# Decay tables, scores and outputs of the retention layer, placed later in the first layer of a two-block transformer

## The chip, the cores and the metric

The kernel runs on one core of one Trainium2 chip. The time is the device time of one execution in microseconds (us), from start to end, without the host. TensorE multiplies matrices into PSUM, VectorE (DVE in the profile) and ScalarE (ACT) work element by element, GpSimd (POOL) does small powers here, and SyncE (SP) issues the DMA loads.

## The reference

Two transformer blocks on 256 rows of 1024 values. Only the first layer of the first block matters here: a retention layer with 6 heads and a memory attention with 4 heads beside it.

```python
h = rms_norm(x, attn_norm_w[layer])
u = h @ w_in[layer]
q, k, v, g = ...                       # 6 heads: q, k 64 wide, v 128 wide, gates 768 wide
o = rms_norm(retention(q, k, v), ret_gn_w[j])
o_main = jax.nn.silu(g) * o.reshape(B, S, MAIN_WIDTH)
...
mkv = memn @ w_mem_kv[layer]           # memory keys and values from a normed memory of 256 rows
o_mem = memory_attention(qc, mk, mv).reshape(B, S, MEM_WIDTH)
x = x + jnp.concatenate([o_main, o_mem], axis=-1) @ w_out[layer]
```

Retention is written in chunks in the reference. The kernel uses its closed form: scores q·k of each head, times a table of decays (powers of that head's gamma by distance, zero where a later chunk is masked), times v. The gates pass a SiLU. Then come a feed-forward network, a second layer with differential attention, and a second block of other mixers.

## The kernel before, in words

All products are made in parts: `unit` loads a weight block of 256 rows (a DMA into a `raw` buffer, of which there are three), ScalarE casts it to a rounded high half `hi` (L328), VectorE subtracts to get the low half `lo` (L213 is the helper `tt`), with four buffers each. `proj` multiplies a block in two half-blocks of six products each (12 products of 512 columns for a block of 512 columns), and before each half-block it calls `tick()`, which moves every running side chain (a Python generator, begun by `start`) one step on. `drain` runs a chain to its end. So the code's order of small work is set by the ticks of the projection beside which it runs. The order in which an engine's instructions are issued in the end is a planner's: it follows the code's order, but a later instruction whose data and buffers are ready can go ahead of an earlier one that waits.

The first layer, `ret_layer`, goes like this. The query/key projection of retention (`proj_T`, columns 0 to 767, in two parts) leaves three tiles of tag T. `setup_rest` loads the remaining constants and x. Then, in the version before, six decay tables of 128 x 384 values (192 KB each) are fetched from the array `small` into tiles of tag L (22 buffers) by `fetch` (L209). The first value projection (columns 768 to 1279) follows; its two results are written by ScalarE into L tiles. The transposed memory, memT, comes in four loads into tiles of tag V (L456; three buffers), each with a scaling into halves (`early`). The second value projection (1280 to 1535) has the memory queries in the same blocks. Beside it runs `products`: for each head two products q·k into one PSUM tile (four such tiles, two tags in turn), and a multiplication with the table on VectorE, in place in the L tile. Both chains are drained behind it.

Next comes `mem_kv(0)`, the memory's key/value projection, and beside it `outputs`: for four groups (two row halves, two sets of three heads) the scores times v into a PSUM tile, a square (ScalarE), a sum, two small steps around a power on GpSimd, and a scaling into a T tile. It is drained, and the gate projections follow (columns 1536 to 2303, four blocks of 512 columns, four of 256); beside them `memory` finishes the key transposes after seven ticks and then makes the memory attention (query transposes, logits, softmax, transposes of the probabilities, values). The gates are multiplied with the outputs, transposed, and go with the memory's result into the output projection; before it, the second layer's memory projection is made, `mem_kv(1)`.

Of the kernel before, what the change touches and what calls it, by code (L numbers as in the profile page):

```python
# [128 lines left out]
class _Builder:  # L129
# [490 lines left out]
    def ret_layer(self):  # L620
        nc, w = self.nc, self.a['w_in'][0]
        hT = self.scaled_T(self.a['xT'], 'attn', 'H')
        qk = []
        for cols in ([(0, 512)], [(512, 256)]):
            for ps in self.proj_T(hT, w, cols):
                e = self.t('T', F32, (P, 2, S))
                (nc.scalar.copy if len(qk) % 2 else nc.vector.tensor_copy)(e, ps)
                qk.append(e)
        self.setup_rest()
        dec = []  # L630
        for h in range(6):
            d = self.t('L')
            self.fetch(d[:, :384], f'dec{h}')
            dec.append(d[:, :384])
        dT = []

        def products():
            for h in range(6):
                s = slice((h % 2) * 64, (h % 2) * 64 + 64)
                f = h // 2  # L640
                q, k = qk[f // 2][s, f % 2, :], qk[(3 + f) // 2][s, (3 + f) % 2, :]
                ps = self.psum()
                self.mm(ps[:, :S], k[:, :P], q)
                self.mm(ps[:, S:S + P], k[:, P:], q[:, P:])
                self.tt(dec[h], ps[:, :384], dec[h])
                dT.append(dec[h])
                if h % 2:
                    yield

        v = [[None, None] for _ in range(2)]  # L650
        a0 = self.proj(hT, w, [(768, 512)])
        ms, r = self.stats(self.x)
        epsms, hr, rv = self.tiny(2), self.tiny(2), self.tiny(2)
        self.ts(epsms, ms, EPS)
        self.ts(hr, r, 0.5)
        self.stt(rv, r, 64.0 ** -0.5, r)
        for t in range(2):
            v[t][0] = self.t('L')
            self.act(v[t][0], a0[t], AF.Copy, scale=rv[:, t:t + 1])
        self.msums = []  # L660
        self.memT = self.scaled_T(self.a['memT'], 'mem', 'Z', self.msums)

        def early():
            for k in range(0, 8, 2):
                yield
                yield
                self.memT[k]

        ea = self.start(early())
        pr = self.start(products())  # L670
        a1 = self.proj(hT, w, [(1280, 256), (2304, 256)])
        for t in range(2):
            v[t][1] = self.t('L')
            self.act(v[t][1][:, :S], a1[t][:, :S], AF.Copy, scale=rv[:, t:t + 1])
        qn = self.mem_q([a1[t][:, S:] for t in range(2)], epsms)
        self.drain(pr, ea)
        on = {}

        def outputs():
            yield  # L680
            last = None
            for t in range(2):
                for hg in range(2):
                    o = self.psum()
                    for hh in range(3):
                        h = hg * 3 + hh
                        for j in range(t + 1):
                            blk = (0 if t == 0 else (P if j == 0 else S))
                            self.mm(o[:, hh * P:(hh + 1) * P], dT[h][:, blk:blk + P],
                                    v[j][h // 4][:, (h % 4) * P:(h % 4 + 1) * P], start=(j == 0), stop=(j == t))  # L690
                    rr = self.head_rms(o[:, :384], 3, P, epsms[:, t:t + 1])
                    if last:
                        last()

                    def last(t=t, hg=hg, o=o, rr=rr):
                        self.ts(rr, rr, hr[:, t:t + 1])
                        e = self.t()
                        self.tt(self.h3(e[:, :384], P), self.h3(o[:, :384], P), self.bc(rr, P))
                        on[t, hg] = e
                    yield  # L700
                    yield
            last()

        out = self.start(outputs())
        mkv0, omT = [], []
        kv = self.mem_kv(0, mkv0)
        self.drain(out)

        def memory():
            yield from kv  # L710
            yield
            yield from self.mem_attn(qn, mkv0, omT)

        mem = self.start(memory())
        sg = {}
        for c, wd in ((0, 512), (1, 256)):
            g = self.proj(hT, w, [(1536 + c * 512, wd)])
            for t in range(2):
                e = self.t('Z')
                self.act(e[:, :wd], g[t], AF.Tanh, scale=hr[:, t:t + 1])  # L720
                self.stt(e[:, :wd], e[:, :wd], 1.0, g[t], ALU.add, ALU.mult)
                sg[t, c] = e
        og = [[None] * 6 for _ in range(2)]
        for t in range(2):
            for hg in range(2):
                e = on[t, hg]
                for lo, hi, c in (((0, 3, 0),) if hg == 0 else ((3, 4, 0), (4, 6, 1))):
                    d = e[:, (lo - 3 * hg) * P:(hi - 3 * hg) * P]
                    base = lo * P - c * 512
                    self.tt(d, d, sg[t, c][:, base:base + (hi - lo) * P])  # L730
                for h in range(3):
                    og[t][hg * 3 + h] = e[:, h * P:(h + 1) * P]
        oT = []

        def transposes():
            yield
            yield from self.to_T(oT, lambda t, f: og[t][f], 6, 'L', lambda f: self.col('ret', f))

        tr = self.start(transposes())
        self.mkv1 = []  # L740
        kv = self.mem_kv(1, self.mkv1)
        self.drain(tr, mem)
        self.start(kv)
        self.xT = self.out_proj(oT + omT, self.a['w_out'][0], order=[6, 7, 0, 1, 2, 3, 4, 5], gname='ffn')
# [949 lines left out]
```

## Time and profile before

| what | value |
|---|---|
| median of 3 runs | 1261.44 us (1261.12 to 1261.72) |
| profiled execution, device time | 1263.25 us |
| profiled execution, span from the first to the last instruction | 1261.5 us |
| TensorE busy | 1239.2 us (98%) |
| VectorE / ScalarE / GpSimd busy | 858.9 / 687.3 / 60.9 us |
| mean granted clock of TensorE | 0.998 |

The times are of runs without a profile, the span and the busy times of the one with. A granted clock of 1.00 is TensorE's 2.4 GHz level, 0.50 its 1.2 GHz level.

### The profile page before, as it was taken

The numbers are of one execution on the slowest core, as the hardware profiler recorded it, in microseconds if no ns is written. First come the engines' busy times: TensorE is split into PE (matmuls) and PEld (weight loads), VectorE is DVE, ScalarE is ACT, GpSimd is POOL, SyncE is SP. The second block draws the span as 40 slices with busy tenths as digits, with TensorE's granted clock in tenths as the row PEclk, the third lists the DMA queues.
The fourth block names the chain that finished last, engine by engine and source line by source line (L and its number), as shares of the span: only waits on it lengthen the run. The fifth ranks groups of instructions, "written<-read, shape, count | busy, mean of one in ns | idle before, by whom it ended". The sixth has DMA issues, their size and how long they took to land.

```text
span 1261.5 us, 18951 instructions
## 1 busy us (share of the span) xinstructions
PE 1239.2 (98%) x7128; PEld 1060.6 (84%) x7128; DVE 858.9 (68%) x1370; ACT 687.3 (54%) x1087; POOL 60.9 (5%) x63
## 2 busy tenths in 40 slices
PE   8999999999999999999999999999999999999997
PEld 7888888888778888888888998878888898888886
DVE  6777777755798677775558896676646665777553
ACT  5655655544576475554466973623554454655442
POOL 0110000000220100000000100111000000000000
PEclk9999999999999999999999999999999999999999
DMA  8745566655554356665663454332666543555662
GB/s 299 227 127 174 171 196 185 190 199 185 182 163 152 121 170 196 186 192 192 192 190 100 149 153 145 116 98 86 182 186 188 176 151 117 177 190 184 189 195 101
DMA packets 146573, 213.62 MB, mean 169 GB/s; under 512 B 15536, under 2 KB 71984, under 8 KB 146480
## 3 DMA queue, kind: packets, MB, share of 16 engines
q1 hardware_dynamic: 145904, 211.34, 53.4%
q8 instruction: 56, 0.92, 0.3%
q0 software_dynamic: 144, 0.52, 0.1%
q10 hardware_dynamic: 432, 0.53, 0.1%
q14 instruction: 37, 0.30, 0.1%
HBM read 210.92 MB, written 1.44 MB: 168 GB/s over the span
## 4 chain that ended last, share of the span: by engine, by line
PE 81%; DVE 8%; DMA 4%; ACT 3%; issue 2%; POOL 1%; SPq 0%; POOLq 0%; DVEq 0%; ACTq 0%
PE acc L235 73%; PE ps L235 6%; DMA raw<-in_w_in_dram 3%; DVE lo L213 2%; PE ps L238 2%; POOL tiny L228 1%; DVE Z L220 1%; ACT T L223 1%; ACT hi L328 1%; DVE T L213 1%; DMA V<-in_mem_2T_dram 1%; ACT L223 0%; DVE tiny L217 0%; DMA T<-dr 0%; DVE L L213 0%
## 5 line engine op out<-in xcount | busy, mean ns | idle before, releaser
L213 DVE TENSOR_TENSOR lo<-raw,hi 128x1024 fp32r<-128x1024 f32 (+1 forms) x393 | 474.4, 1210 | 286.9 <-ACT hi L328 285.9
L328 ACT CAST hi<-raw 128x1024 fp32r<-128x1024 f32 (+1 forms) x393 | 408.3, 1040 | 400.7 <-PE acc L235 322.3
L235 PE MATMUL acc<-H,hi 128*128 128x512 f32 (+1 forms) x1696 | 471.6, 348 | 1.7 <-ACT hi L328 0.9
L235 PE MATMUL acc<-H,lo 128*128 128x256 f32 x1328 | 369.5, 280 | 3.4 <-DVE lo L213 3.4
L235 PEld LDWEIGHTS acc<-H,hi 128*128 128x128 f32 x1696 | 294.6, 189 | 47.5 <-ACT hi L328 1.6
L235 PEld LDWEIGHTS acc<-H,lo 128*128 128x128 f32 x1328 | 250.4, 189 | 5.3 <-DVE lo L213 4.7
L235 PE MATMUL acc<-hi,H 128*128 128x512 f32 (+1 forms) x672 | 217.4, 395 | 0.8 <-ACT hi L328 0.8
L235 PE MATMUL acc<-hi,Z 128*128 128x512 f32 x544 | 175.5, 395 | 0.1
L235 PE MATMUL acc<-hi,L 128*128 128x512 f32 x512 | 160.7, 391 | 0.0
L235 PEld LDWEIGHTS acc<-hi,H 128*128 128x128 f32 x672 | 125.4, 189 | 28.2 <-issue 2.8
L235 PE MATMUL acc<-lo,H 128*128 128x512 f32 (+1 forms) x336 | 131.2, 390 | 0.0
L235 PEld LDWEIGHTS acc<-hi,Z 128*128 128x128 f32 x544 | 102.1, 188 | 21.1 <-ACT Z L249 0.5
L235 PEld LDWEIGHTS acc<-hi,L 128*128 128x128 f32 x512 | 96.1, 188 | 19.8
L235 PE MATMUL acc<-lo,Z 128*128 128x512 f32 x272 | 106.4, 391 | 0.0
L235 PE MATMUL acc<-lo,L 128*128 128x512 f32 x256 | 99.7, 389 | 0.0
L228 POOL TENSOR_TENSOR tiny<-tiny,constants 128x2 f32<-128x2 f32 (+4 forms) x41 | 45.3, 1109 | 978.8 <-DVE tiny L217 903.6
L235 PEld LDWEIGHTS acc<-lo,H 128*128 128x128 f32 x336 | 63.8, 190 | 12.1 <-issue 0.7
L235 PEld LDWEIGHTS acc<-lo,Z 128*128 128x128 f32 x272 | 51.2, 188 | 9.8
L235 PEld LDWEIGHTS acc<-lo,L 128*128 128x128 f32 x256 | 48.1, 188 | 9.7
L414 ACT COPY T<-acc 128x256 f32<-128x256 f32 x120 | 44.2, 369 | 14.4 <-PE acc L235 11.2
L213 DVE TENSOR_TENSOR T<-acc,T 128x256 f32<-128x256 f32 x120 | 44.9, 415 | 0.0
L223 ACT ACTIVATE H<-ps,constants 128x256 fp32r<-128x256 f32 x56 | 24.6, 471 | 12.8 <-DVE H L220 9.8
(224 smaller groups left out, 1052.8 us busy)
## 6 DMA issues: line engine op xcount, KB each, us to landing
raw<-in_w_in_dram SPq DMA_DIRECT2D x91, 512.0 KB, 3.6
raw<-in_w_gate_up_dram SPq DMA_DIRECT2D x176, 256.0 KB, 3.2
raw<-in_mlp_w_dram SPq DMA_DIRECT2D x64, 512.0 KB, 3.7
raw<-in_w_down_dram SPq DMA_DIRECT2D x44, 512.0 KB, 3.6
raw<-in_w_out_dram SPq DMA_DIRECT2D x24, 512.0 KB, 3.7
raw<-in_w_in_dram SPq DMA_DIRECT2D x42, 256.0 KB, 3.6
raw<-in_w_mem_kv_dram SPq DMA_DIRECT2D x8, 512.0 KB, 4.2
raw<-in_xattn_wk_dram SPq DMA_DIRECT2D x8, 512.0 KB, 4.5
```

The source lines that it names most:

```text
L213: return (eng or self.nc.vector).tensor_tensor(out=out, in0=a, in1=b, op=op)
L220: self.nc.vector.scalar_tensor_tensor(out=out, in0=a, scalar=s, in1=b, op0=op0, op1=op1)
L223: self.nc.scalar.activation(out, in_, f, scale=scale, bias=bias, **k)
L228: self.nc.gpsimd.tensor_tensor(out=out, in0=in_, in1=self.c('mhalf')[:, :n], op=ALU.pow)
L235: self.nc.tensor.matmul(out, lhsT, rhs, start=start, stop=stop, skip_group_check=True)
L238: self.nc.tensor.transpose(out, in_, self.ident[:in_.shape[0], :in_.shape[0]])
L328: nc.scalar.copy(hi[:, k, :W], raw[:, k, :W])
L414: self.nc.scalar.copy(out[:, a, :], accs[a][:, 1, :])
```

## The change

The fetches of the six tables move behind the second value projection and the memory queries. The scores (`products`) no longer run beside the second value projection but beside `mem_kv(0)`. The outputs no longer run beside `mem_kv(0)` but, started behind it, beside the gate projections, and are drained after these. No instruction is added or removed.

```diff
         self.setup_rest()
-        dec = []
-        for h in range(6):
-            d = self.t('L')
-            self.fetch(d[:, :384], f'dec{h}')
-            dec.append(d[:, :384])
-        dT = []
+        dec, dT = [], []
...
         ea = self.start(early())
-        pr = self.start(products())
         a1 = self.proj(hT, w, [(1280, 256), (2304, 256)])
...
         qn = self.mem_q([a1[t][:, S:] for t in range(2)], epsms)
-        self.drain(pr, ea)
+        self.drain(ea)
+        for h in range(6):
+            d = self.t('L')
+            self.fetch(d[:, :384], f'dec{h}')
+            dec.append(d[:, :384])
...
-        out = self.start(outputs())
+        pr = self.start(products())
         mkv0, omT = [], []
         kv = self.mem_kv(0, mkv0)
-        self.drain(out)
+        self.drain(pr)
+        out = self.start(outputs())
...
                 sg[t, c] = e
+        self.drain(out)
```

## Rows read from the trace of the kernel before

**Rows 1.** The page, part 1: busy time, share of the span, instructions.
```profile
PE 1239.2 (98%) x7128; PEld 1060.6 (84%) x7128; DVE 858.9 (68%) x1370; ACT 687.3 (54%) x1087; POOL 60.9 (5%) x63
```
**Rows 2.** Busy time by stretch: length, each engine, granted clock, DMA share, GB/s.
```profile
16.00:24.78 8.78, 8.78 (x75) 8.65 (x74) 3.47 (x10) 4.87 (x12) 0.70 (x1) 1.00 1.05 371
24.78:29.91 5.13, 4.37 (x29) 3.35 (x29) 4.55 (x8) 2.38 (x3) 0.00 (x0) 1.00 0.88 326
29.91:33.32 3.41, 3.41 (x10) 2.64 (x9) 3.41 (x6) 3.29 (x7) 0.00 (x0) 0.50 0.76 193
33.32:52.30 18.98, 18.98 (x85) 15.73 (x84) 11.82 (x14) 11.67 (x16) 0.00 (x0) 1.00 0.77 237
52.30:67.96 15.66, 15.66 (x91) 13.59 (x90) 13.21 (x28) 8.45 (x15) 6.47 (x5) 1.00 0.51 160
67.96:79.81 11.85, 11.85 (x58) 9.80 (x58) 6.95 (x18) 4.50 (x9) 3.53 (x4) 1.00 0.36 109
79.81:89.71 9.90, 8.60 (x71) 7.74 (x69) 9.18 (x23) 6.56 (x18) 0.00 (x0) 1.00 0.42 129
```
**Rows 3.** Timeline of TensorE, 24.75 to 33.4 us: start, duration, instruction, idle before.
```profile
24.78 2.48 PE L235 MATMUL ps<-T,T 64*128 64x256 f32 x20
28.02 0.73 PE L235 MATMUL acc<-hi,H 128*128 128x512 f32 x2 [0.76 <-ACT hi L328]
28.69 0.92 PE L235 MATMUL ps<-T,T 64*128 64x256 f32 x4
...
33.25 0.44 PE L235 MATMUL acc<-hi,H 128*128 128x512 f32 x1
```
**Rows 4.** Timeline of ScalarE, 21 to 30 us.
```profile
26.93 1.04 ACT L328 CAST hi<-raw 128x1024 fp32r<-128x1024 f32 x1 [4.57 <-DMA raw<-in_w_in_dram]
28.27 1.05 ACT L328 CAST hi<-raw 128x1024 fp32r<-128x1024 f32 x1 [0.30 <-DMA raw<-in_w_in_dram]
```
**Rows 5.** Timeline of the SP queue, 16 to 34 us.
```profile
16.23 4.42 SPq L209 DMA_DIRECT2D L<-in_small_dram  x6
21.10 2.20 SPq L322 DMA_DIRECT2D raw<-in_w_in_dram  x3
```
**Rows 6.** The fetches of L209 between 15 and 30 us, the decay tables.
```profile
DMA to landing us min/median/max: 5.2/6.5/6.7
```
**Rows 7.** Timeline of the SP queue, 48 to 54 us.
```profile
50.33 2.95 SPq L322 DMA_DIRECT2D raw<-in_w_in_dram  x2
53.33 0.46 SPq L456 DMA_DIRECT2D V<-in_memT_dram  x1
```
**Rows 8.** Timeline of ScalarE, 50 to 54 us.
```profile
52.77 0.47 ACT L223 ACTIVATE L<-acc,tiny 128x256 f32<-128x256 f32 x1 [0.50 <-PE acc L235]
53.14 0.38 ACT L223 ACTIVATE V<-acc 128x256 f32<-128x256 f32 x1
```
**Rows 9.** Groups of VectorE by shape, 16 to 33.4 us: count, busy us, mean ns.
```profile
L213 DVE TENSOR_TENSOR lo<-raw,hi 128x1024 fp32r<-128x1024 f32 x3 | 3.6, 1217 | 0.3 <-ACT hi L328 0.3
L213 DVE TENSOR_TENSOR L<-ps,L 128x384 f32<-128x384 f32 x6 | 3.0, 550 | 0.2 <-PE ps L235 0.2
...
L627 DVE COPY T<-acc 128x512 f32<-128x512 f32 x2 | 1.4, 692 | 3.3 <-PE acc L235 3.3
```
**Rows 10.** The fetch of L209 at 250.7 us, a load alone.
```profile
DMA to landing us min/median/max: 3.6/3.6/3.6
```
**Rows 11.** Groups by shape, 52.3 to 67.96 us: the outputs' work.
```profile
L235 PE MATMUL ps<-L,L 128*128 128x128 f32 x36 | 4.7, 274 | 0.0
...
L469 DVE TENSOR_REDUCE tiny<-V 128x3 f32<-128x384 f32 x4 | 2.2, 545 | 0.0
...
L213 DVE TENSOR_TENSOR T<-ps,tiny 128x384 f32<-128x384 f32 x3 | 1.7, 552 | 0.0
L217 DVE TENSOR_SCALAR tiny<-tiny,tiny 128x3 f32<-128x3 f32 x6 | 1.2, 226 | 0.8 <-POOL tiny L228 0.8
```
**Rows 12.** Waits of TensorE, 67.96 to 92 us: us in total, times, longest.
```profile
PE ps L238 <- DVE T L217: 1.0, 1, 1.0
```

## Prediction

> **What bounds the kernel now.** I read the page first. TensorE is busy 98% of the span, VectorE 68% [rows 1], so a change can only win where TensorE waits or is slowed, and only lose where it makes TensorE wait. The table of stretches then shows where, around this change. Before 24.78 us the second query/key projection runs without a hole while the DMA engines are full (share 1.05). From 24.78 to 29.91 TensorE is busy 4.37 of 5.13 us, and from 29.91 to 33.32 its granted clock is 0.50, the 1.2 GHz level. From 33.32 to 79.81 nothing is idle, and from 79.81 to 89.71 it is busy 8.60 of 9.90 [rows 2].
>
> The timeline of TensorE shows the bad stretch in detail. The scores of heads 0 to 4 (20 instructions) fill it from 24.78, then TensorE idles 0.76 us; two products of the value projection start at 28.02, head 5's scores at 28.69, and only at 33.25 does the projection run at its later pace [rows 3]. What is late is the first weight block of that projection: ScalarE's cast of it starts at 26.93, after 4.57 us of waiting for its DMA; the next one follows 1.34 us later [rows 4]. The SP queue says why it is late: after the last constants, the six decay tables are issued (4.42 us for the six issues), and the three weight blocks only from 21.10 on [rows 5]. Each table takes 5.2 to 6.7 us to land [rows 6].
>
> How much is lost there? Of the 8.47 us from 24.78 to 33.25, the scores hold TensorE for 2.48 and 0.92 [rows 3]. Eleven projection products fit before 33.25; at the pace of the next stretch, 85 instructions in 18.98 us or 0.223 each [rows 2], they would need 2.46. So 5.86 us of work took 8.47: **2.61 us are lost**. 0.76 of it is the idle time; the 3.41 us at half clock give up to half of themselves, 1.70; the rest, 0.15, is changes between kinds of work.
>
> **The change, part by part.** *Tables.* Whether they really load later is a matter of buffers: they need no data. The code takes them from tag L, now behind the four value tiles of that tag. In this trace a tile seems to get a buffer only after every earlier tile of its tag has one: the last quarter of memT (tag V) is issued at 53.33 [rows 7], just after ScalarE began, at 53.14, the second of two V tiles that stand before it in the code [rows 8], though SP had been free for it earlier. By that, no table can be issued before the last value tile is written, now 52.77 [rows 8].
>
> Six tables of 192 KB, at 1.34 us for a 512 KB block [rows 4], are 6 x 0.50 = 3.0 us of DMA time, taken out from before the first value block. Its cast then starts at 23.9 instead of 26.93, and ends after 1.05 at 24.95. The low half takes VectorE 1.22 us [rows 9], so it is there at 26.2, or 26.9 if the copy of the last query/key tile (0.69) [rows 9] goes first. TensorE is free at 24.78, so it waits 0.2, does the two products that need no low half (0.45, to 25.4), and has a hole of 0.8 to 1.5 us. The scores need no table, only VectorE's multiplication behind them does, so the first four heads can fill the hole as they fill it now (they took 2 x 0.78 us, below). Hole with filling 0.1, without 1.5; with the first 0.2 I take 0.3 lost. Nothing is then late: the blocks land 1.34 apart and each feeds 12 products, 2.7 us. No half clock follows, since the holes that came before it are gone. Head 5 runs alone now, 0.92; if head 4 does too, the other two pairs take (2.48 - 0.92) / 2 = 0.78 each. Heads 4 and 5 as a pair would save 2 x 0.92 - 0.78 = 1.06; I take 0.4, since they may be split again. Startup gain: 2.61 - 0.3 + 0.4 = **2.7 us**, between 1.1 (hole of 1.5 unfilled, no pairing) and 3.5.
>
> *Scores and tables in the memory key/value stage (52.30 to 67.96).* VectorE's six multiplications of 0.55 [rows 9] move here, 3.3 us, while the outputs' work, below, leaves; VectorE was busy 13.21 of 15.66 [rows 2], so it has room. On SP the six issues go behind the memory weights; gate blocks are issued from 50.33 [rows 7] and first used at 67.96, so 3.0 us of DMA time more is hidden. Were that cover gone, it would cost up to those 3.0. The new wait: heads 4 and 5 need a score buffer back, there are four, and these are released by the multiplication with a table. A table issued at the last value tile, 0.5 us into the stage, lands 3.6 us later at best (a load from the same array that runs alone [rows 10]) or 6.7 at worst [rows 6]; with 0.55 more, 4.6 to 7.7 into the stage. The code puts heads 4 and 5 at the third half-block, 12 x 0.223 = 2.7 into it. Left there, TensorE would stand 1.9 to 5.0. The order of issue follows readiness, as head 5's place behind two projection products shows [rows 3]; the error to be feared is that of a misjudged landing, as the 0.76 us at 28.02. I take 0.4, with bounds 0 and 5.0.
>
> *Outputs into the gates (67.96 to 89.71).* The 36 small products (4.7 us of TensorE) and, for each of four groups, a square on ScalarE, and a reduction (0.55), two small steps (0.23 each) and a multiplication (0.55) on VectorE [rows 11], move from one full stage to another. TensorE's part costs the same in either. VectorE's part is 4 x 1.56 = 6.2 us; VectorE is busy 6.95 of 11.85 and then 9.18 of 9.90 [rows 2], and the stage grows by 4.7, so it fits, if it comes early. The code puts the groups at every second half-block, the last of them one step before memory attention's transposes. There VectorE is crowded, and TensorE's wait of 1.04 us for the softmax scaling [rows 12] is already VectorE's doing. The last group, 1.56 us, falls into this crowd; about as much there, the gate multiplications, can wait, and the second memory projection's blocks can fill a hole of TensorE. Best, the present 1.04 is filled; worst, all 6.2 us push the attention. I take 0.1 lost.
>
> Sum: -2.7 + 0.4 + 0.1 = **-2.2 us**. It is made against the profiled execution, span 1261.5 and time 1263.25, which lies 1.8 above the median 1261.44 of the runs without profile. I put the same difference on the median: **1259.2 us**. This is just short of 0.2% (2.5 us), about what a measurement of this kernel can tell from no change.
>
> **A rule against the change.** The table of six landings above 5 us, at a DMA share of 1.05, says that loads issued early here take turns from the weights [rows 2, 6]. The Trainium skill, DMA: Bandwidth & Descriptors, section Rules for kernel authors, says the opposite of what the change does: issue a DMA early, compute, and wait on it late, so that its fixed cost overlaps. By that rule the gain would be eaten by the wait for tables; that is the second rival, and the sum would be +0.4 instead of -2.2.
>
> **Rivals.**
> 1. *The gates' hole closes too.* The startup gain stays 2.7, no wait for tables comes, and the 1.04 us before the softmax transposes are filled: -3.7, 1257.7, between -3.2 and -4.2 by how heads 4 and 5 fall. For it: TensorE's pending work there grows. Against: VectorE's queue there has no idle share to speak of. Chance 0.15.
> 2. *The tables come late.* TensorE reaches heads 4 and 5 and stands 1.9 to 5.0 us, middle 3.0: -2.7 + 3.0 + 0.1 = +0.4, 1261.8, between 1260.7 and 1263.8. For it: the distance between 2.7 and 4.6 us. Against: the order so far followed readiness. Chance 0.08.
> 3. *The tables don't move.* Buffers of L are free early; if my reading of rows 7 and 8 is wrong, SP issues the tables where it does now and nothing at the start changes: 1261.4, within 0.5. Chance 0.09.
> 4. *Slower: VectorE's queue in the gates.* Its place is the chain from the last output group through key copy, query copy and the softmax's reductions to the transposes TensorE waits for. Every group of 1.56 us that runs there instead of earlier lengthens that wait; two groups undo the gain, and with all four it is 6.2 - 2.7 = +3.5, 1264.9. For it: 9.18 of 9.90 busy. Against: the first groups come eight half-blocks earlier. Chance 0.06.
>
> **How the numbers follow.** The forecast has 0.62, with its own range of -1.0 to -3.4 (1258.0 to 1260.4); its part beyond -2.5 is 0.28. Faster: 0.28 + 0.15 = 0.43. Within 0.2%: the other 0.34 + 0.08 + 0.09 = 0.51. Slower: 0.06. The range for 8 in 10 runs from 1257.2 (first rival's far end) to 1262.0 (third rival, and the second's lower half); outside are the fourth, half of the second, and tails.
>
> **What would show it.** Right: the timeline of SP has the tables behind the memory weights, near 48 us; the cast of the first value block starts near 24; no stretch near 30 us has a granted clock of 0.50; the gates begin earlier and end about 2 us earlier. Wrong: tables still at 16 us; TensorE waits for a table-fed multiplication in the key/value stage; the wait for the softmax scaling grows past 2 us, or the granted clock halves elsewhere.

## The result and the profile after

The changed kernel takes 1270.25 us (median of 6, 1267.42 to 1273.83), the kernel before 1261.65 in the same comparison (6 runs): ratio 1.0068, interval 1.0057 to 1.0079, so 8.6 us slower. The forecast was 1259.2 with a range up to 1262.0, and 0.06 for slower. The profiled execution took 1269.07 us, its span is 1267.4. Of the six runs, the three slowest (1271.43 to 1273.83) show a mean granted clock of 0.993 to 0.994, the other three, the profiled one among them, 0.996 to 0.997.

The windows of the kernel after, in the columns of [rows 2], cut at its own stages: the start of the first value projection, the memory key/value stage (49.42 to 70.33), the gates (70.33 to 98.36).

```profile
25.83:33.30 7.47, 7.47 (x34) 5.67 (x33) 6.27 (x10) 5.69 (x9) 0.00 (x0) 1.00 0.93 313
33.30:49.42 16.12, 16.12 (x74) 13.06 (x72) 10.22 (x11) 10.73 (x16) 0.00 (x0) 1.00 0.76 229
49.42:58.95 9.53, 6.09 (x30) 4.44 (x30) 5.38 (x13) 3.60 (x7) 2.50 (x2) 1.00 0.90 298
58.95:65.78 6.83, 6.83 (x18) 4.80 (x17) 4.07 (x8) 1.04 (x1) 0.00 (x0) 0.50 0.18 43
65.78:70.33 4.55, 4.55 (x21) 3.73 (x20) 2.23 (x3) 1.44 (x2) 0.00 (x0) 1.00 0.34 120
70.33:86.65 16.32, 16.32 (x97) 14.22 (x96) 10.24 (x27) 6.62 (x13) 6.18 (x6) 1.00 0.27 82
86.65:98.36 11.71, 8.77 (x71) 8.01 (x69) 10.45 (x27) 6.58 (x18) 0.85 (x1) 1.00 0.39 111
```

The start is what the prediction wanted: no idle time, clock at 1.00, where [rows 2] have 0.76 us idle and 3.41 us at 0.50. The key/value stage is where it went wrong: 3.44 us idle and 6.83 us at half clock, of which about half, 3.4, is lost (an estimate: the work in it would have taken half the time at 1.00). The gates have 2.94 us idle, against 1.30 in [rows 2]. The timeline of TensorE shows the place in the key/value stage.

```profile
51.02 0.93 PE L235 MATMUL ps<-T,T 64*128 64x256 f32 x8
...
53.59 0.39 PE L235 MATMUL acc<-lo,Z 128*128 128x512 f32 x1
57.42 0.92 PE L235 MATMUL ps<-T,T 64*128 64x256 f32 x4 [3.44 <-DVE L L213]
58.27 0.73 PE L235 MATMUL acc<-hi,Z 128*128 128x512 f32 x2
58.84 0.53 PE L235 MATMUL acc<-lo,Z 128*128 128x512 f32 x1
```

The releaser is VectorE's line 213 on an L tile, the multiplication with a table. So the next question is why that came at 57. The timeline of the SP queue, and then the view of line 209 in this stretch, with the landing times of its six fetches:

```profile
47.29 2.80 SPq L322 DMA_DIRECT2D raw<-in_w_in_dram  x2
50.13 0.46 SPq L456 DMA_DIRECT2D V<-in_memT_dram  x1
50.65 3.10 SPq L209 DMA_DIRECT2D L<-in_small_dram  x6
```
```profile
DMA to landing us min/median/max: 5.6/5.7/5.8
```

And VectorE, then ScalarE, in the same stretch:

```profile
56.42 0.48 DVE L220 SCALAR_TENSOR_TENSOR Z<-V,constants,Z 128x256 fp32r<-128x256 f32 x1 [4.08 <-ACT Z L223]
56.82 0.55 DVE L213 TENSOR_TENSOR L<-ps,L 128x384 f32<-128x384 f32 x1
```
```profile
55.88 0.91 ACT L223 ACTIVATE Z<-V,constants 128x256 fp32r<-128x256 f32 x2 [5.22 <-DMA V<-in_memT_dram]
```

The tables did move, as the reading of [rows 7, 8] had it: behind the last quarter of memT, 50.65 in place of 16.23 [rows 5]. The first lands at 50.65 + 5.7 = 56.35. VectorE's first multiplication starts at 56.82, because its in-order queue also stood for memT's last quarter; without that it could have started some 0.5 earlier. It ends at 57.37, TensorE goes on at 57.42. The two things behind the wait are nearly equal in time, and the tables are enough for it. In the stage's own time, the first table was there 6.9 us after its start (the prediction had 4.1 to 7.2 for that) and TensorE was through with all that stood ahead of head 4's scores at 4.6 (53.98). The prediction had 2.7 for that: it counted twelve products of the projection and left out the scores of heads 2 and 3 (0.93 us at 51.02).

### The profile page after: what moved, and what is told of

Same layout as the page of the kernel before. It is cut to its first block, busy times and chain, and to the rows that moved or that the text cites. A ratio compares the mean times of both kernels' runs of the same rounds, so it can differ in the third digit from the quotient of the medians.

```text
span 1267.4 us, 18955 instructions
## 1 busy us (share of the span) xinstructions
PE 1242.4 (98%) x7128; PEld 1063.2 (84%) x7128; DVE 859.0 (68%) x1370; ACT 688.0 (54%) x1087; POOL 60.3 (5%) x63
## 4 chain that ended last, share of the span: by engine, by line
PE 82%; DVE 7%; DMA 4%; ACT 3%; issue 2%; POOL 1%; SPq 0%; POOLq 0%; ACTq 0%; DVEq 0%
PE acc L235 74%; PE ps L235 6%; PE ps L238 2%; DVE lo L213 2%; DMA raw<-in_w_in_dram 2%; POOL tiny L228 1%; ACT hi L328 1%; DVE T L213 1%; DVE Z L220 1%; ACT T L223 1%; DMA V<-in_memT_dram 0%; DVE tiny L217 0%; DMA raw<-in_w_mem_kv_dram 0%; DVE L L213 0%; DMA T<-dr 0%
## 5 line engine op out<-in xcount | busy, mean ns | idle before, releaser
L213 DVE TENSOR_TENSOR lo<-raw,hi 128x1024 fp32r<-128x1024 f32 (+1 forms) x393 | 474.5, 1210 | 285.6 <-ACT hi L328 284.6
L213 DVE TENSOR_TENSOR T<-acc,T 128x256 f32<-128x256 f32 x120 | 44.9, 416 | 0.0
```

The costliest lines, as they stand in the source:

```text
L213: return (eng or self.nc.vector).tensor_tensor(out=out, in0=a, in1=b, op=op)
```

## The experiments

Four kernels separate the three moves; the rest measure single terms. All differences are medians against the kernel before in the same comparison (1260.79 to 1261.91).

### The three moves, taken apart

Outputs beside the gates alone, in the kernel before:

```diff
-        out = self.start(outputs())
...
-        self.drain(out)
+        out = self.start(outputs())
...
+        self.drain(out)
```

> The kernel before with one part of the change: the outputs run beside the gates; tables and scores stay early. Theory A (the loss is the wait for the tables in the key/value stage and the half clock behind it, the gates only add what the changed kernel's two waits there, 2.21 and 0.74 us against 0.25 and 1.04, show): about 1.7 us slower than before, no wait over 1 us between 45 and 70 us. Rival B (the outputs beside the gates are the main cause): 5 us or more slower. The prediction's own term: 0.1 us.

Measured: 1263.95, +2.7 us, 1.0022 [1.0012, 1.0031].

The changed kernel with its tables fetched behind the results of the first value projection:

```diff
             self.act(v[t][0], a0[t], AF.Copy, scale=rv[:, t:t + 1])
+        for h in range(6):
+            d = self.t('L')
+            self.fetch(d[:, :384], f'dec{h}')
+            dec.append(d[:, :384])
         self.msums = []
...
         self.drain(ea)
-        for h in range(6):
-            d = self.t('L')
-            self.fetch(d[:, :384], f'dec{h}')
-            dec.append(d[:, :384])
```

> The changed kernel, with the table fetches one projection earlier, behind the results of the first value projection, so that they should be issued near 38 us instead of 50.65. Theory A: the 3.44 us wait of TensorE and the 6.83 us at half clock both go, the startup gain of about 2 stays, the gates' 1.7 stay: within 1 us of before. Rival B: still 4 us or more slower than before. Rival C (late is not the tables but the last quarter of memT, on which ScalarE waits 5.22 us and behind which the multiplications are queued): the wait near 57 us stays above 2 us.

Measured: 1263.55, +2.3, 1.0018 [1.0010, 1.0027].

The kernel before with only that: tables behind the first value projection, scores and outputs as before:

> The kernel before with the table fetches alone moved behind the results of the first value projection; scores and outputs stay where they were. Theory A: the startup gain without its prices, 2 us faster than before (2.7 by the prediction's term); the cast of the first value block starts near 24 us. If the startup stall was not made by the tables: same as before within 0.5 us.

Measured: 1264.33, +3.1, 1.0025 [1.0016, 1.0034]. A miss: it was to be faster.

The changed kernel with the tables fetched where they were before:

> The changed kernel, with the table fetches back at their old place before the first value projection. Theory A: no wait near 57 us, the startup stall back, the gates' price: 1.5 to 2.5 us slower than before. Rival D (the scores beside the memory projection cost by themselves, by their place and the clock): 4 us or more slower.

Measured: 1262.74, +1.5, 1.0011 [1.0003, 1.0019]. In its trace the scores did not move: with the tables there early, the planner has them at the start, where they were before.

```profile
25.62 2.48 PE L235 MATMUL ps<-T,T 64*128 64x256 f32 x20
```

So this kernel differs from the one before by the outputs alone, and the reading that scores beside the memory projection cost by themselves is not put to the test by it. The kernel with the tables behind the first value projection has them beside the memory projection.

These put the 8.6 us together: tables fetched behind the second value projection instead of the first, 8.6 - 2.3 = **6.3**; behind the first instead of at the start, which moves the scores too, 2.3 - 1.5 = **0.8** (the two intervals overlap, so this is not told from nothing); everything else, which is the outputs in the gates, **1.5** (2.7 by the first of these kernels; the intervals overlap). In the waits of TensorE from 24 to 100 us, of the changed kernel and then of the one with the tables behind the first value projection, the wait for L213 is there and gone, while that for L529 stays:

```profile
PE ps L235 <- DVE L L213: 3.4, 1, 3.4
PE ps L235 <- DVE T L529: 2.2, 1, 2.2
PE ps L238 <- DVE T L217: 0.7, 1, 0.7
```
```profile
PE ps L235 <- DVE T L529: 2.9, 1, 2.9
PE ps L238 <- DVE T L217: 0.7, 1, 0.7
PE ps L235 <- ACT T L559: 0.2, 1, 0.2
```

3.44 us of wait and 3.4 lost at half clock are 6.8 by the profile, 6.3 by the runs. The profile is of an execution 1.2 us below the changed kernel's median; where the slower runs have their further half clock isn't known. The kernel with only the tables moved shows the same wait once more, where its scores stand, and half clock behind it (3.41 us, 45.51 to 48.92); its wait:

```profile
PE ps L235 <- DVE L L213: 2.3, 1, 2.3
```

The wait and half of the 3.41 us are 4.0, more than the 3.1 that it lost; so its start may have gained about 0.9, an estimate from one profile.

In the kernels with all of it moved and earlier tables, memT's last quarter is issued later than in the changed one (51.50 with the tables behind the first value projection, 52.72 with them at the start, against 50.13), and there is no such wait. So memT is not its cause.

### The wait for the tables by itself

The changed kernel, tables as late as ever, the scores of heads 4 and 5 three half-blocks later:

```diff
                 if h % 2:
                     yield
+                if h == 3:
+                    for _ in range(3):
+                        yield
```

> The changed kernel with the scores of heads 4 and 5 put three half-blocks later, behind tables that land as late as before. If what costs most is TensorE standing at those scores because their buffers come free only with the first multiplications with a table: the wait of 3.4 us falls below 1 us, no half clock follows in the memory key/value stage, and the time falls by 4 to 6 us to 1264 to 1266. If instead the late memory load and VectorE's queue behind the tables hold the projection itself, the wait moves to one of its products and the time stays at 1268 or above.

Measured: 1265.74 (6 runs, 1263.99 to 1266.99), +4.6, so 4.0 us less than the change's 8.6. The waits:

```profile
PE ps L235 <- DVE T L529: 2.7, 1, 2.7
PE ps L235 <- DVE L L213: 0.4, 1, 0.4
```

The wait shrank from 3.4 to 0.4 and the half clock in this stage is gone, with the tables as late (issued from 50.42 on, 50.65 in the changed kernel). Between 53.98, where the changed kernel stands, and 57.02 TensorE ran products of the projection without idle time, so there was other work that was ready:

```profile
56.70 0.39 PE L235 MATMUL acc<-hi,Z 128*128 128x512 f32 x1
57.02 0.92 PE L235 MATMUL ps<-T,T 64*128 64x256 f32 x4
```

What was wrong was the distance between scores and tables. It stays 2.3 us above the kernel with the earlier tables; in its profiled execution two stretches of 3.41 us at half clock stand later (85.08 and 754.09), at up to 1.7 us each; whether that is so in its other runs isn't known.

### What the start was worth

The kernel before without the table loads:

```diff
-            self.fetch(d[:, :384], f'dec{h}')
+            nc.gpsimd.memset(d[:, :384], 1.0)
```

> The kernel before with the six tables set to 1.0 by GpSimd in place of being loaded, so the decay weighting is left out; everything else stays. It gives the most that freeing the start from the table loads can bring, with the scores where they are. By the prediction's startup term (idle 0.76 plus 1.70 of half clock plus 0.15): 2 to 2.6 us faster than before, 1258.6 to 1259.2. By the rival reading that the half clock near 30 us belonged to the one profiled execution (two kernels with the same start show 0.43 and 0.48 us idle and the clock at 1.00 there): 0.3 to 0.8 us faster, 1260.4 to 1260.9, no idle ahead of the first value product.

Measured: 1260.00 against 1261.17, 0.9992 [0.9983, 1.0000]: 1.2 us faster by the medians, 1.0 by the ratio, by the interval between 0 and 2.1. And the kernel before with the fetches one weight block later, called from inside the first value projection:

```diff
+        def tables():
+            for h in range(6):
...
-        a0 = self.proj(hT, w, [(768, 512)])
+        a0 = self.proj(hT, w, [(768, 512)], meanwhile=tables)
```

> The kernel before with the six table loads one place later in the code: behind the first weight block of the first value projection instead of ahead of it. Scores and outputs stay. If the idle time ahead of that projection (0.4 to 0.8 us) is all that can be had at the start, and the scores fill it as they come: no idle there, 0.4 to 1.0 us faster than before, 1260.2 to 1260.8, the same as without any table loads (1260.0). If the second and third block now come late behind the tables, or the scores wait for them as they did with tables behind the whole projection: a new wait of 1 to 2.5 us between 27 and 36 us, and 1261.5 to 1264.

Measured: 1261.13 against 1260.79, 1.0001 [0.9992, 1.0010]. Its start has no idle time and no half clock in the profile, and the scores no new wait; still nothing is gained. Part of the reason is seen in kernels whose start is the same as before's. The window from the scores on, in the kernel with the outputs moved alone, then in the changed one with early tables:

```profile
25.76:33.50 7.74, 7.26 (x41) 5.75 (x41) 7.44 (x12) 5.31 (x8) 0.00 (x0) 1.00 0.73 246
```
```profile
25.62:33.30 7.68, 7.25 (x41) 5.75 (x41) 7.42 (x12) 5.28 (x8) 0.00 (x0) 1.00 0.72 247
```

The clock is 1.00 in both, the idle time 0.48 and 0.43. Over the eleven profiles with tables loaded early, that of before among them, half clock stands at the start in three. So the 1.70 us belonged to some executions, and the profiled one, 1.8 us above the median, was one of these. The other two lie 1.0 and 2.4 us above the medians of their kernels.

The idle time saved is also paid back: scores that filled the start's hole go into a stage without one. With early tables the 24 products took 2.48 + 0.92 = 3.40 us in two groups [rows 3]; in the kernel with tables behind the first value projection they are in four groups, 0.70 + 0.92 + 0.93 + 1.51 = 4.06:

```profile
26.09 0.70 PE L235 MATMUL ps<-T,T 64*128 64x256 f32 x2
...
48.27 0.92 PE L235 MATMUL ps<-T,T 64*128 64x128 f32 x6
...
50.71 0.93 PE L235 MATMUL ps<-T,T 64*128 64x256 f32 x8
...
53.27 1.51 PE L235 MATMUL ps<-T,T 64*128 64x256 f32 x8
```

0.66 us more against 0.43 saved, and at the end of the key/value stage this kernel is 0.65 us later than the one with early tables (63.01 and 62.36), though its value projection began 3.1 earlier (25.45 and 28.54). The groups account for 0.23 of that; the rest isn't traced. Nor is the number of groups the whole of it: eight products took 0.93 at 50.71 and 1.51 at 53.27.

### What the outputs cost beside the gates

The wait that grew is the one for L529, VectorE's copy of the transposed queries, ahead of the logits. In VectorE's timeline of the changed kernel:

```profile
87.90 0.22 DVE L217 TENSOR_SCALAR tiny<-tiny,tiny 128x3 f32<-128x3 f32 x1
88.03 0.28 DVE L213 TENSOR_TENSOR T<-T,Z 128x128 f32<-128x128 f32 x1
89.08 0.23 DVE L217 TENSOR_SCALAR tiny<-tiny,tiny 128x3 f32<-128x3 f32 x1 [0.77 <-POOL tiny L228]
89.22 0.68 DVE L529 COPY T<-ps 128x512 f32<-128x512 f32 x1
```

What it copies is there well before, since TensorE's transposes of the queries end at 86.90:

```profile
86.30 0.60 PE L238 MATMUL ps<-constants,Z 128*128 128x128 f32 x4
```

The copy stands behind the last output group's second small step, which waits for GpSimd's power. To take the copy out of this queue, it goes to ScalarE (`nc.scalar.copy` in `mem_attn`), in the kernel before as a control and in the changed one with early tables:

> The kernel before with one instruction moved: the copy of the transposed memory queries out of PSUM goes from VectorE to ScalarE. It is the control for the next kernel. TensorE waits 0.25 us ahead of the logits there, so at most 0.3 us faster; the wait for the softmax scaling (1.0 us) is VectorE's and stays: 1260.9 to 1261.4.

> The changed kernel with its tables loaded at the old early place (1262.74 us, TensorE waits 2.2 us ahead of the logits) and the same one copy on ScalarE. If the outputs in the gates cost what they cost because VectorE reaches that copy late, behind the outputs' small steps and their round trip to GpSimd: the wait falls below 1 us and the time by 1.5 to 3 us, to 1259.7 to 1261.2. If the wait is for something else (the key copy, ScalarE's own queue, the outputs' buffers), it stays above 1.5 us and so does the time, 1262 to 1263.5.

Measured: 1261.26 (+0.1, as expected) and 1262.35 (+1.2, against +1.5 with the copy on VectorE: no gain that can be told). In the second the waits ahead of the logits fell to 0.4 and 0.3, but the wait for the softmax scaling came in their place:

```profile
PE ps L238 <- DVE T L217: 1.5, 1, 1.5
PE acc L235 <- ACT hi L328: 0.8, 1, 0.8
PE ps L235 <- DVE tiny L217: 0.4, 1, 0.4
PE ps L235 <- DVE T L213: 0.3, 1, 0.3
```

So the copy is where VectorE's lateness shows first, and not its cause. Next, the groups one half-block apart, to have them over before the crowd (one `yield` less in `outputs`), with early tables and with tables behind the first value projection:

> The changed kernel with its tables loaded at the old early place (1262.74 us), and the four output groups one half-block apart in the gates instead of two, so that the last of them stands some four half-blocks earlier. If the cost of the outputs in the gates is that the last groups fall into VectorE's crowd just ahead of the memory attention: TensorE's wait ahead of the logits falls from 2.2 us to about the 0.25 us of the kernel before, and the time by 1 to 2 us, to 1260.7 to 1261.7. If the stage is simply too full for VectorE wherever they stand, the waits and the time stay, 1262 to 1263.5.

> The same closer outputs in the kernel whose tables are loaded behind the first value projection (1263.55 us; waits of 2.9 and 0.75 us in the gates). The same two readings: 1261.3 to 1262.5 if the place of the last groups is the cost, 1263 to 1264.5 if it is the amount. It is the best form that the change can have with tables behind a value projection; if the startup gain of the prediction (2.7 us) were real on top, it would reach 1259 to 1260.

Measured: 1265.06 (+4.3) and 1265.48 (+4.7). Both readings missed: it got 2.4 to 2.8 us worse. The last group's products did come earlier in the first of them (71.24 in place of 75.16), but VectorE's copy came later (82.40 in place of 81.25). Its timeline shows it standing for GpSimd in each group:

```profile
73.32 0.23 DVE L217 TENSOR_SCALAR tiny<-tiny,tiny 128x3 f32<-128x3 f32 x1 [0.96 <-POOL tiny L228]
...
75.96 0.23 DVE L217 TENSOR_SCALAR tiny<-tiny,tiny 128x3 f32<-128x3 f32 x1 [1.03 <-POOL tiny L228]
...
79.14 0.23 DVE L217 TENSOR_SCALAR tiny<-tiny,tiny 128x3 f32<-128x3 f32 x1 [0.96 <-POOL tiny L228]
```

These waits are 3.9 us in all, against 3.7 with the groups two half-blocks apart, so they don't tell why closer is worse.

So the power was left out (`head_rms` then returns the mean square itself), in the kernel with early tables and in the one with closer groups:

```diff
-                    rr = self.head_rms(o[:, :384], 3, P, epsms[:, t:t + 1])
+                    rr = self.head_rms(o[:, :384], 3, P, epsms[:, t:t + 1], False)
```

> The changed kernel with its tables loaded at the old early place (1262.74 us), and the power of the outputs' norm on GpSimd left out: the outputs are scaled by their mean square instead of its inverse root. One small GpSimd step of 0.85 us in each of the four groups goes, and VectorE no longer waits for it (3.7 us in all in the gates, against 1.4 in the kernel before). If these waits at the head of VectorE's queue are what makes the outputs dear in the gates: the wait ahead of the logits falls from 2.2 us to below 1 and the time by 1 to 2 us, to 1260.7 to 1261.7, the kernel before's. If it is the amount of VectorE's own work, waits and time stay at 1262 to 1263.5.

> The kernel with the outputs one half-block apart (1265.06 us), and the same power left out. If VectorE's waits for GpSimd are why standing closer made it slower (3.02 us ahead of the logits): 2.5 to 4.5 us faster, 1260.5 to 1262.5, and then closer is no worse than two half-blocks apart. If closer is worse because more of VectorE's work is due at once: at most 1 us faster, 1264 to 1265.

Measured: 1260.99 (-0.9 against before; 0.9989 [0.9980, 0.9998]) and 1260.77 (-1.1; 0.9997 [0.9988, 1.0006]), 2.4 and 5.4 us under the kernels with the power by medians, 2.8 and 4.7 by the ratios. Neither has a wait for L529 any more; the first one's waits are

```profile
PE ps L238 <- DVE T L217: 0.7, 1, 0.7
PE acc L235 <- ACT hi L328: 0.3, 1, 0.3
```

VectorE has as much work of its own as with the power, so it is the waits for the power that make the outputs dear there, at either distance. Last, the same without leaving anything out: the row's factor is folded into the step ahead of the power, so that VectorE meets the power's result one instruction later, at the scaling.

```diff
+        self.ts(c1, ms, 4.0 / P)
+        self.stt(c2, ms, 4.0 * EPS, ms)
...
-        self.ts(ss, ss, 1.0 / d, ALU.mult, epsms, ALU.add)
+        self.ts(ss, ss, 1.0 / d if scale is None else scale, ALU.mult, epsms, ALU.add)
...
-                    rr = self.head_rms(o[:, :384], 3, P, epsms[:, t:t + 1])
+                    rr = self.head_rms(o[:, :384], 3, P, c2[:, t:t + 1], c1[:, t:t + 1])
...
-                        self.ts(rr, rr, hr[:, t:t + 1])
```

> The changed kernel with its tables loaded at the old early place, and the outputs' last small step on VectorE (the factor 0.5/rms of the row, behind GpSimd's power) folded into the step before the power by scaling the mean square and its epsilon by the row's constants; the result is the same. VectorE then meets GpSimd's power only at the scaling of the outputs, a group later. If standing at the head of the queue is the cost: like the kernel without the power, 1 to 2.5 us under its 1262.74 us, 1260.2 to 1261.7, and no wait above 1 us ahead of the logits. If the planner puts the scaling where it must wait as well: 1262 to 1263.

> The kernel before with the same fold. There the outputs stand in the memory key/value stage, where VectorE's waits for GpSimd (1.4 us in all) are covered by TensorE's full queue. If it is the place that makes them dear: no change against the kernel before, within 0.5 us. If four small steps fewer are worth something by themselves: 0.5 to 1.5 us faster.

> The kernel with the outputs one half-block apart (1265.06 us) and the same fold. If VectorE's stand for GpSimd is the cost: 2.5 to 4.5 us faster, 1260.5 to 1262.5, like the same kernel without the power. If the scaling, now due one half-block behind its power, takes over the wait: 1263 to 1265.

Measured: 1261.08 (+0.2, 1.0006 [0.9997, 1.0015]), 1261.48 (+0.6, 1.0008 [0.9999, 1.0016]) and 1262.48 (+1.6, 1.0011 [1.0002, 1.0019]). Beside the gates the fold brings the outputs down to what the kernel before takes; where they stood before it brings nothing. With closer groups it helps by 2.7 us and leaves a wait of 2.5 ahead of the logits: there the scaling takes over the stand. VectorE's waits for GpSimd with L213, from 62 to 100 us, without the power, then with the fold (groups two half-blocks apart), then with fold and closer groups:

```profile
DVE T L213 <- POOL tiny L228: 1.7, 2, 0.9
```
```profile
DVE T L213 <- POOL tiny L228: 4.6, 5, 1.0
```
```profile
DVE T L213 <- POOL tiny L228: 5.6, 6, 1.0
```

So with the fold and the wider distance VectorE still stands 2.9 us at three of the four scalings, and yet the cost is gone: TensorE's wait for the copy is 0.7 in place of 2.2. What went is the last group's stand of 0.77 right ahead of the copy, and four small steps; the copy starts at 79.60, in place of 81.25. With closer groups all four scalings stand ahead of the copy. No kernel that computes the whole came out below the kernel before.

## Why the prediction was wrong

**Where the tables go** (buffers of tag L, SP's order) was right, to the instruction in front of them. The rival in which they don't move fell.

**The tables' wait, "I take 0.4", is the step that failed.** The bounds were right: "Left there, TensorE would stand 1.9 to 5.0" and it stood 3.44, in part by luck: it came to the scores 4.6 us into the stage, not 2.7, and went on at 8.0, not at 4.6 to 7.7. What was wrong is the choice inside them: "The order of issue follows readiness". On the chip it did not: TensorE stood at these scores while products of the projection were ready, as the kernel with the later scores shows. The order is the planner's; what it took the tables' landing to be isn't on record. In the changed kernel and in the one with only the tables moved, TensorE reached the scores 3.4 and 2.3 us before their buffer came free. The idle time of 0.76 in [rows 3], cited there as an error to be feared, was the sign of this and was priced too low. The second rival had the mechanism, with 3.0 for the wait, and 0.08 for its chance.

**Half clock behind that wait had no term.** 6.83 us at 0.50 stand behind it, which made 3.44 into 6.8. "No half clock follows" was said of the start, and held there; for the tables' wait nothing was put down, and the second rival left it out as well. The prediction had seen half clock behind an idle time of 0.76 and counted it as a loss there; the same price was due on its own wait.

**The startup gain, 2.7, was not there.** Its mechanism was right (no idle time, no half clock, value projection at 25.83 in place of 28.02), its size wrong: the loads taken away altogether give 1.0, moved behind the first block 0, and moved behind the whole projection between -0.8 (by the runs, not told from nothing) and 0.9 (the estimate from the kernel with only the tables moved). 1.70 of the 2.61 came from a stretch that this execution had and most of those profiled lack, while the sum was put on a median 1.8 us below that execution. The remainder was eaten at least in part by the scores' new place: 4.06 us in four groups instead of 3.40 in two, in a stage with no hole.

**The outputs in the gates, 0.1, cost 1.5 to 2.7.** The fourth rival named the place (VectorE's queue up to the softmax) and the sign, but priced VectorE's busy time, 1.56 a group. What decided was time in which VectorE is not busy: it stands for GpSimd's power, 3.7 us over four groups, with the query copy behind. Not all of the 3.7 has a price: with the fold 2.9 of it remain and the cost is 0.2; the stand right ahead of the copy and the small steps are what went. In the kernel before, the same waits are 1.4 us over the four groups (0.8 of it in [rows 11]). The Trainium skill, PSUM — Partial Sum Buffer, section Engine vs sequencer instructions, says that the queues of ScalarE, VectorE and GpSimd are strictly first in, first out; the rows agree: the copy at 89.22, whose data had been there, follows a wait of 0.77 for something else.

**The hidden DMA time, 3.0,** was right: no wait of TensorE for a gate block appears. The rule set against the change (the Trainium skill, DMA: Bandwidth & Descriptors, section Rules for kernel authors: issue early, wait late) is borne out in its sign, with 6.3 us between late and earlier issue, of which about half is the wait and half the lower clock behind it. That issue at the very start is better than behind the first value projection isn't shown: the 0.8 between them is within the intervals.

Together: +0.8 for the start with the scores' new place where -2.7 was forecast, 6.3 for the tables where 0.4 was, 1.5 for the outputs where 0.1 was. That the three add to 8.6 follows from how they were formed; that the tables' wait is the largest is shown by two separate edits, earlier tables (-6.3) and later scores (-4.0).

## What to carry to other kernels

A stall's price in a profile of one execution holds for the median only if that execution is at the median: where it is slower by about the size of the half clock in it, count the idle time alone. When a load moves behind a stage, write down when it lands against when the fixed order of issue reaches its first use, and if the second comes first, take the wait in full, and a lower clock behind it as a possible price more. When small work moves to a stage where an in-order engine is busy, look for the round trips that stand ahead of what the bottleneck engine waits for (here 0.77 to 1.03 us for each power on GpSimd), and don't price the engine's busy time alone.

## What the runs showed of the hardware that was not expected

- Half clock follows some idle times and not others of the same length. Behind 3.44 us idle in the changed kernel it stood for 6.83 us; at 2.83 in the kernel with the outputs moved it stood for 6.83 (82.62 to 89.45, so from shortly before the idle time's end at 83.25), behind 2.21 in the one with early tables for 3.41; behind the same 2.21 in the changed kernel's gates and behind 2.90 in the one with tables behind the first value projection there was none. At the start, idle times of 0.76 and 0.82 were followed by it and one of 0.95 was not.
- The same 24 score products cost 3.40 us in two groups and 4.06 in four; eight of them took 0.93 us in one place and 1.51 in another.
- A table took 5.6 to 5.8 us to land at a DMA share of 0.90 in its stretch, about what it takes at the start, where the share is 1.05 [rows 2, 6]; the load alone, 3.6 [rows 10], was no guide for the later place.
